# All input projections by seven products, in stages of 1536 and 1024 columns, with one function each for silu and gelu and a planner that alternates late and early passes

## The chip, the cores and the metric

The kernel runs on one core of a Trainium2 chip. Five engines work side by side on that core: PE (TensorE, matrix products into PSUM), VectorE (DVE in the profile), ScalarE (ACT), GpSimd (POOL) and SyncE (SP), which here issues nearly all transfers between DRAM and SBUF. Each engine takes its own instructions in order and waits on semaphores for the others. The metric is the device time of one execution in microseconds; lower is better.

## The reference

One layer of a decoder: 1024 tokens, model width 2048, all in float32. In short:

```python
h = rmsnorm(x, ln_g)
P = h @ w_in                       # 2048 x 6672
g_u, g_v, g_z, d_q, d_k, d_v, d_z, d_a, d_b, c_q, c_z = split(P)
A = gelu(g_u) * (tril(W_s) @ layernorm(gelu(g_v)) + b) * silu(g_z)       # 4 groups x 128
q, k, v = silu(causal_conv(d_q, d_k, d_v))                               # 8 heads x 128 each
B = rmsnorm(gated_delta_rule(l2norm(q), l2norm(k), v, decay(d_a), sigmoid(d_b))) * silu(d_z)
C = softmax(c_q @ mk.T) @ mv * silu(c_z)      # 4 heads, 256 memory tokens, mk, mv = rmsnorm(mem) @ w_mem_kv
y = rmsnorm(x + concat(A, B, C) @ w_out, final_g)
```

The delta rule is a scan over the tokens in chunks, with a triangular inverse for each chunk and a 128x128 state for each head.

## The kernel before

**Products.** A float32 operand is split by `split_to` (line 457) into a rounded part `hi` (ScalarE) and the rest `lo` (VectorE), and a product is three fast products, hi·hi, hi·lo and lo·hi (`triple`, line 480). Tokens are handled as two halves of 512 (`hf`), so a product has 128 columns of weights (or tokens) as its stationary operand and 512 columns moving.

**Stages, in program order.**
1. The memory projection: `w_mem_kv` in 16 steps of k, with the norm of memory and, in between, the norm of x's first half (`prep`, line 572): square sums on ScalarE, a VectorE multiply by row factor and gain, transposes on PE, then split into `ahi`/`alo` (four quarters each, resident) and stored as `h0_d`. The gain was copied to all partitions by `spread_gain` (line 567): four products of a row of ones.
2. Plain products for q, k and v of heads 0 to 3 (`project`, `project_first`, lines 891 and 906): for each head and each token half 16 steps of k with 3 products, the result going straight into the convolution. Weights come in pieces of 128x512; their `lo` is kept in DRAM for the second half (`low_d`). `project_first` does its 48 products as two token halves of 256 columns each, so that it can start before all tokens are normed. Norm and transposes of x's second half (`prep1`, `keep_rows`) and the sums of the two halves (`left_sums`) are jobs on the list `todo`, started one by one behind later products.
3. Five pairs of 512-column blocks (`pairs`: q/k of heads 4 to 7; z of the delta heads; v of heads 4 to 7 with the gating's v; the gating's u and z; attention's z and q) by `seven` (line 1341): Strassen's scheme in Winograd's form. Inputs are the two token halves and the two halves of the model width on one side, the two halves of the width and the two column blocks on the other. Seven products, in the order 2, 1, 6, 5, 3, 7, 4 (the "keys"), each over 8 steps of k and 4 column tiles, replace eight. Keys 2 and 1 take the first token half as it is; 5, 6, 7 and 3 take sums of token halves, kept in DRAM; 4 takes the second half. The weight differences are made on the fly by VectorE (`rights_made`, `minus`). Four PSUM banks hold one product; after a key they are copied or added out (`takes`) while the next key begins.
4. The output projection: two more such pairs, interleaved.

**Side work.** For each pair of heads and token half: `front` (convolution, silu, norms, the chunk's two 128x128 tables), `inverse` (62 small VectorE operations for up to four fronts at once), `levels` (block inverse on PE), `values`, `scan_step` and `heads_out` (together `back`). Heads 0 to 3 did this in one go during stage 2; for heads 4 to 7 `front` stored its tiles in DRAM (`late_d`) and `front_late` read them back some stages later. It uses the PSUM banks `dn0` to `dn3`.

**Functions.** `tanh_gate` and `gelu2` (lines 785 and 792) made silu and gelu from tanh with extra VectorE steps; exp and tanh are the only other looked-up functions.

**Order.** Every call is recorded by `Plan` (line 62) as an operation with an engine, a price and its dependences. `lay` simulates the engines and picks, on each, the ready operation with the lowest key; `latest` sets due times backwards from the order found; three rounds are made and the order with the earliest simulated end is written out. All instructions therefore carry line 312 in the profile, and one goes by tile names.

Of the kernel before, what the change touches and what calls it, by code (L numbers as in the profile page):

```python
# [9 lines left out]
F32 = mybir.dt.float32  # L10
# [28 lines left out]
GELU_C = math.sqrt(2.0 / math.pi)  # L39
GELU_A = 0.044715  # L40
# [8 lines left out]
class Op:  # L49
    __slots__ = ("eng", "fn", "args", "kw", "cls", "idx", "cost", "lat", "nbytes", "lock", "n", "succ", "ready", "at",  # L50
                 "lead", "tail", "wait")
# [11 lines left out]
class Plan:  # L63
# [3 lines left out]
    DMA_RATE = 300.0  # L67
    DMA_FIXED = 1600.0
    SWITCH = 250.0
    SPREAD, PASSES = 1.5, 2  # L70
# [111 lines left out]
    def price(self, o, name, outs, ins):  # L182
# [6 lines left out]
        o.nbytes = o.lock = 0  # L189
        o.lat = 0.0  # L190
        if name == "dma_start":
            o.cost = {"sp": 490.0, "act": 100.0, "pool": 800.0}[o.eng]
            rows = math.prod(out.shape[:-1])
            o.nbytes = max(4 * math.prod(out.shape), 512 * rows)
            src = ins[0]
# [11 lines left out]
        elif o.eng == "act":  # L207
            o.cost = (165.0 if psum else 200.0) + 0.82 * n + (105.0 if pointer else 0.0)
# [14 lines left out]
    def lay(self, key):  # L223
# [5 lines left out]
        dma = 0.0  # L229
# [5 lines left out]
        while left:  # L235
# [14 lines left out]
            head = self.ops[heapq.heappop(now[e])[1]]  # L250
            for o in (head, *head.tail):
# [6 lines left out]
                if o.lock:  # L258
                    held[e] = end
                free[e] = end - min(self.OVERLAP[e], 0.5 * o.cost)  # L260
# [17 lines left out]
        return max(free.values())  # L278
# [21 lines left out]

    def issue(self):
        key, best = [o.cls for o in self.ops], None
        for _ in range(self.PASSES + 1):
            end = self.lay(key)
            if best is None or end < best[0]:
                best = end, [o.at for o in self.ops]
            key = self.latest()
        for o, o.at in zip(self.ops, best[1]):
            pass
        self.ops.sort(key=lambda o: (o.at, o.idx))  # L310
        for o in self.ops:
            o.fn(*o.args, **o.kw)  # L312
# [3 lines left out]
def kernel(  # L316
# [84 lines left out]
    ahq = [C([P, NT, 4, P], f"ahi{q}", F32R) for q in range(NQ)]  # L401
    alq = [C([P, NT, 4, P], f"alo{q}", F32R) for q in range(NQ)]
    for t in (*ahq, *alq):
        R.users[t.tensor.name] = []
    ahi = [ahq[k // 4][:, :, k % 4] for k in range(KT)]
    alo = [alq[k // 4][:, :, k % 4] for k in range(KT)]
    wraw = Ring("wraw", 2, [P, 2 * HT])
    whi = Ring("whi", 2, [P, 2 * HT], dt=F32R)
    wlo = Ring("wlo", 2, [P, 2 * HT], dt=F32R)
    kvraw = [*wraw.bufs]  # L410
    kvhi, kvlo = [*whi.bufs], [*wlo.bufs]
    for r in (wraw, whi, wlo):
        r.bufs = [b[:, i * HT : (i + 1) * HT] for b in r.bufs for i in range(2)]
    whi.bufs.append(C([P, HT], "whi4", F32R))
    wlo.bufs.append(C([P, HT], "wlo4", F32R))
    ring = {t: Slots(t, 4, [P, HT]) for t in ("kT", "qT", "vs", "kd", "ai")}
    ring |= {t: Slots(t, 2, [P, 2 * HT]) for t in ("inv", "gt")}
    ring["ut"] = Ring("ut", 2, [P, 2 * HT])
    ring["zg"] = Ring("zg", 2, [P, 2 * HT])
    zgb = ring["zg"].bufs  # L420
    ring["zg"].bufs = [b[:, i * HT : (i + 1) * HT] for b in zgb for i in range(2)]
# [19 lines left out]
    hT_d = DT([KT, P, HT], "hTd")  # L441
# [18 lines left out]

    def raw_piece(src, cls=4):
        raw = wraw()
        v = raw if src.ndim == 2 else raw.rearrange("p (k c) -> p k c", k=src.shape[1])
        with rank(cls):
            Q.dma_start(v, src)
        return raw

    def split_piece(raw):
        hi, lo = whi(), wlo()
        with rank(2):  # L470
            split_to(hi, lo, raw, V)
        return hi, lo
# [27 lines left out]
    def row_tiles(tag):  # L500
        if tag in ("inv", "gt", "ut"):
            return [b[:, i * HT : (i + 1) * HT] for b in (ring[tag](), ring[tag]()) for i in range(2)]
        return [ring[tag]() for _ in range(4)]

    gb = [ring["zg"]() for _ in range(4)]
    kvraw += [ring["ut"]() for _ in range(2)]
    mem_rows = [row_tiles("kT"), row_tiles("qT")]
# [14 lines left out]
    def load_x(tt, tag, after=(None,) * 4):  # L522
        x_rows[tt] = row_tiles(tag)
# [6 lines left out]
    mrow = rows[0:16]  # L530
    with rank(2):
        load_mem(0)
        S.dma_start(mrow, mem_norm_g[0].rearrange("(c p) -> c p", p=P))
        for c in range(4):
# [1295 lines left out]
```

## Time and profile before

| | |
|---|---|
| median of 3 runs (lowest, highest) | 1628.9 us (1628.83, 1635.46) |
| profiled execution | 1628.64 us |
| its span, first to last instruction | 1626.9 us |
| PE, VectorE, ScalarE busy | 1610.1, 1321.4, 1020.9 us |
| TensorE clock granted | 0.998 of full speed |
| bytes moved by transfers | 419.44 MB |

How to read it: `PE` are products, `PEld` their weight loads, which overlap. A group row has line, engine, operation, out<-in by tile names (digits left out), shape and count, then busy time in us and the mean duration in ns, then the idle time of the engine ahead of the group and what ended it. Products overlap in the pipeline, so their durations add up to more than the time they take; the distance between two starts is the time that one costs. A window row has, for each engine, busy time and count in that stretch, then the granted clock, the mean busy share of the 16 DMA engines and the rate in GB/s. A wait row has the total in us, how often, and the longest.

### The profile page before, as it was taken

The numbers are of one execution on the slowest core, as the hardware profiler recorded it, in microseconds if no ns is written. First come the engines' busy times: TensorE is split into PE (matmuls) and PEld (weight loads), VectorE is DVE, ScalarE is ACT, GpSimd is POOL, SyncE is SP. The second block draws the span as 40 slices with busy tenths as digits, with TensorE's granted clock in tenths as the row PEclk, the third lists the DMA queues.
The fourth block names the chain that finished last, engine by engine and source line by source line (L and its number), as shares of the span: only waits on it lengthen the run. The fifth ranks groups of instructions, "written<-read, shape, count | busy, mean of one in ns | idle before, by whom it ended". The sixth has DMA issues, their size and how long they took to land.

```text
span 1626.9 us, 25678 instructions
## 1 busy us (share of the span) xinstructions
PE 1610.1 (99%) x8570; PEld 1350.2 (83%) x8570; DVE 1321.4 (81%) x2288; ACT 1020.9 (63%) x2235; POOL 100.2 (6%) x139
## 2 busy tenths in 40 slices
PE   8999999999999999999999999999999999999997
PEld 6988888888888888888888888888888888888886
DVE  5865796948879869899999898878768897778875
ACT  6957674676755356967776545766667774444355
POOL 0001100010110000100100100000000000000001
PEclk9999999999999999999999999999999999999999
DMA  8978996887886857689877986989768889688646
GB/s 275 272 229 246 289 275 197 248 246 251 282 271 222 285 200 239 206 279 349 293 234 232 327 260 191 292 294 312 262 208 267 297 288 329 200 276 293 213 148 233
DMA packets 316847, 419.44 MB, mean 258 GB/s; under 512 B 51822, under 2 KB 140583, under 8 KB 316715
## 3 DMA queue, kind: packets, MB, share of 16 engines
q1 hardware_dynamic: 315010, 414.65, 79.0%
q0 software_dynamic: 1088, 2.10, 0.4%
q8 instruction: 67, 1.10, 0.3%
q10 hardware_dynamic: 616, 1.07, 0.2%
q14 instruction: 66, 0.53, 0.1%
HBM read 334.33 MB, written 82.87 MB: 256 GB/s over the span
## 4 chain that ended last, share of the span: by engine, by line
PE 98%; DMA 1%; ACT 0%; DVE 0%; issue 0%; ACTq 0%; DVEq 0%; SPq 0%
PE acc L312 75%; PE dn L312 23%; DMA kT<-in_w_in_dram 0%; DMA ut<-in_x_dram 0%; DMA hTd<-tn 0%; DMA kT<-in_mem_dram 0%; ACT y L312 0%; DVE ut L312 0%; DVE kT L312 0%; DVE kd L312 0%; DVE inv L312 0%; ACT vs L312 0%; ACT whi L312 0%; ACT gt L312 0%; ACTq L312 0%
## 5 line engine op out<-in xcount | busy, mean ns | idle before, releaser
L312 PE MATMUL acc<-ahi,whi 128*128 128x512 f32 (+1 forms) x1152 | 442.6, 393 | 0.2
L312 PE MATMUL acc<-alo,whi 128*128 128x512 f32 (+1 forms) x1152 | 440.9, 392 | 0.0
L312 PE MATMUL acc<-ahi,wlo 128*128 128x512 f32 (+1 forms) x1152 | 404.8, 393 | 0.0
L312 PEld LDWEIGHTS acc<-ahi,wlo 128*128 128x128 f32 x1152 | 216.3, 188 | 41.8
L312 PEld LDWEIGHTS acc<-alo,whi 128*128 128x128 f32 x1152 | 216.4, 188 | 40.6
L312 PEld LDWEIGHTS acc<-ahi,whi 128*128 128x128 f32 x1152 | 216.4, 188 | 40.5 <-ACT whi L312 0.9
L312 PE MATMUL acc<-ahi,zh 128*128 128x512 f32 x736 | 222.6, 395 | 0.0
L312 ACT CAST whi<-wraw 128x512 fp32r<-128x512 f32 (+1 forms) x170 | 136.9, 807 | 118.3 <-PE acc L312 91.5
L312 DVE TENSOR_TENSOR alo<-raws,ahi 128x1024 fp32r<-128x1024 f32 x131 | 159.7, 1220 | 37.3 <-ACT ahi L312 35.9
L312 ACT CAST ahi<-raws 128x1024 fp32r<-128x1024 f32 x131 | 137.4, 1050 | 65.5 <-PE dn L312 27.8
L312 DVE TENSOR_TENSOR wlo<-wraw,whi 128x1024 fp32r<-128x1024 f32 (+1 forms) x138 | 134.8, 979 | 40.3 <-ACT whi L312 36.1
L312 PEld LDWEIGHTS acc<-ahi,zh 128*128 128x128 f32 x736 | 136.6, 188 | 26.6
L312 PE MATMUL acc<-ahi,zl 128*128 128x512 f32 x368 | 129.2, 394 | 0.0
L312 DVE TENSOR_TENSOR ahi<-y,ahi 128x1024 fp32r<-128x1024 f32 x65 | 79.3, 1219 | 17.6 <-ACT ahi L312 17.6
L312 ACT CAST ahi<-y 128x1024 fp32r<-128x1024 f32 x65 | 68.2, 1050 | 36.7 <-PE acc L312 26.6
L312 PEld LDWEIGHTS acc<-ahi,zl 128*128 128x128 f32 x368 | 69.1, 188 | 13.4
L312 ACT CAST zh<-wraw 128x1024 fp32r<-128x1024 f32 x36 | 37.8, 1051 | 40.8 <-PE acc L312 17.1
L312 PE MATMUL dn<-wlo,ahi 128*128 128x512 f32 x152 | 59.1, 389 | 0.0
L312 PE MATMUL dn<-whi,ahi 128*128 128x512 f32 x152 | 59.0, 389 | 0.0
L312 PE MATMUL acc<-whi,ahi 128*128 128x512 f32 x144 | 56.1, 392 | 0.0
L312 PE MATMUL acc<-wlo,ahi 128*128 128x512 f32 x144 | 55.9, 391 | 0.0
L312 DVE TENSOR_TENSOR wlo<-y,whi 128x1024 fp32r<-128x1024 f32 x34 | 41.4, 1219 | 14.9 <-ACT whi L312 14.8
(408 smaller groups left out, 3152.7 us busy)
## 6 DMA issues: line engine op xcount, KB each, us to landing
wraw<-in_w_in_dram SPq DMA_DIRECT2D x86, 512.0 KB
raws<-sd SPq DMA_DIRECT2D x74, 512.0 KB
wraw<-in_w_in_dram SPq DMA_DIRECT2D x96, 256.0 KB
y<-in_w_in_dram SPq DMA_DIRECT2D x42, 512.0 KB
y<-sd SPq DMA_DIRECT2D x38, 512.0 KB
wraw<-in_w_out_dram SPq DMA_DIRECT2D x32, 512.0 KB
raws<-h0d SPq DMA_DIRECT2D x27, 512.0 KB
low<-wlo SPq DMA_DIRECT2D x32, 256.0 KB
```

The costliest lines, as they stand in the source:

```text
L312: o.fn(*o.args, **o.kw)
```

## The change

- **Products.** The plain products are gone. q, k and v of heads 0 to 3, then of heads 4 to 7, then z of the delta heads with the gating's v are three stages of 1536 columns by `seven`: two blocks of 512 and two of 256 side by side, six column tiles and six PSUM banks, weight pieces of 128x1536. The last two pairs and the output projection keep 1024 columns.
- **Start.** The first stage takes `ahi`/`alo` as resident operands for keys 2 and 1; its first two steps of key 2 go as two token halves (`first=2`). Key 2 of the second stage is computed right behind (`ahead`) and kept in DRAM. Norm, transposes and sums of x's second half are now one piece of work, `prep1`, ranked as background; it reads the first half back from `h0_d` in short rows and stores the sums so too.
- **Norm.** The gain is a column (`lcol`) and VectorE applies it behind the transpose; `spread_gain` is gone.
- **Side work.** All eight heads store their front tiles and read them back (`late_d`, `gt_d` for all). The decay tables' exponentials move out of the fronts into `decays` and go through DRAM (`e_d`, `ecs`). Fronts and scan share two PSUM banks, later one each, where they had up to four. Transposes of q and k, and of two heads' outputs, go out singly instead of together.
- **Functions.** silu is `AF.Silu`, gelu `AF.Gelu_apprx_tanh`, with no factors to undo.
- **Order.** The planner knows function tables (a price for a change), short-row transfers and a lead limit on SP, and makes eleven rounds: five early passes, and six with keys from `late`, which lays the work out backwards.

The core of the diff:

```diff
-    DMA_RATE = 300.0
+    DMA_RATE = 340.0
-    SPREAD, PASSES = 1.5, 2
+    FIRST, SPREAD, PASSES, STRETCH, AHEAD = 4, 1.75, 6, 1.25, 2000.0
+    TABLE, HOLD = 1300.0, 6000.0
...
-        for _ in range(self.PASSES + 1):
-            end = self.lay(key)
+        for n in range(self.FIRST + self.PASSES + 1):
+            end = self.lay(key, hold)
...
-            key = self.latest()
+            key, hold = self.latest() if n < self.FIRST else self.late(preds), self.HOLD
...
-            V.scalar_tensor_tensor(xq[q], xq[q], r, gb[q], op0=ALU.mult, op1=ALU.mult)
+            V.tensor_scalar(xq[q], xq[q], r, None, op0=ALU.mult)
...
+        with rank(min(R.cls, 1.5)):
+            V.tensor_tensor(out=tok(o), in0=tok(tp), in1=bc(lcol[q], P), op=ALU.mult)
...
     def prep1(i):
-        load_x(NT + i, "ut")
-        prep(NT + i, lambda q, tp: keep_rows(hT_d, q, i, tp), over(scan_banks))
+        for q in range(2):
+            a, b, c, d, e = (pieces() for _ in range(5))
+            for t, k in ((c, q), (d, q + 2)):
+                Q.dma_start(tok(t), quads(h0_d, k, i))
...
+            V.tensor_tensor(out=e, in0=a, in1=b, op=ALU.add)
+            V.tensor_tensor(out=a, in0=c, in1=a, op=ALU.subtract)
+            V.tensor_tensor(out=c, in0=e, in1=c, op=ALU.subtract)
+            V.tensor_tensor(out=d, in0=d, in1=c, op=ALU.subtract)
+            with rank(4.5):
+                for n, t in ((1, c), (0, e), (3, d), (2, a)):
+                    Q.dma_start(quads(hs_d[n], q, i), tok(t))
+                Q.dma_start(quads(hT_d, q, i), tok(b))
...
-        t = ring["tn"]()
-        S.activation(t, o, AF.Tanh)
-        V.scalar_tensor_tensor(o, t, 1.0, o, op0=ALU.add, op1=ALU.mult)
+        S.activation(o, o, AF.Silu)
...
+    zv = ((HT, (C_DZ + HT, C_DZ)), (HT // 2, (C_V, C_V + HT // 2)))
+    NA = 1
+    def others():
+        for cs, d in zip((heads_of(NJ), zv)[:NA], yu_d):
+            ahead(cs, d)
+    project_stage(heads_of(0), to_heads(0), left=held_left, first_yu=early, first=2, beside=beside, then=others)
+    decays(1, ab1)
...
     with rank(2.6):
-        gdrs = [front(p, hf) for hf in range(2) for p in range(NJ // 2, NJ)]
+        gdrs = [front(p, hf, scan_banks) for hf in range(2) for p in range(2)]
+    project_stage(heads_of(NJ), to_heads(NJ), made=yu_d[0] if NA > 0 else None)
+    inv = inverse(gdrs, "a", 1.9)
+    front_sets = over([own_set])
+    scan_banks, work = [dnr.bufs[0]] * 2, over(dnr.bufs[0:1])
...
+        for hf in range(2):
+            for n in range(2):
+                back_of(n, hf, inv[hf * 2 + n])
+                gdrs.append(front(2 + n, hf, [dnr.bufs[1]] * 2))
...
+    project_stage(zv, gated, made=yu_d[1] if NA > 1 else None)
+    inv = inverse(gdrs, "b", 1.9)
...
+    scan_banks, work = dnr.bufs[0:2], over(dnr.bufs[2:3])
     with rank(2.6):
         for hf in range(2):
-            for p in range(NJ // 2, NJ):
+            for n in range(2):
+                back_of(2 + n, hf, inv[hf * 2 + n])
```

944 lines of the change are left out of this document (487 added, 457 removed).

## The prediction

> **What bounds the kernel now.** I read the page first: span, busy times, the chain that ended last.
>
> ```profile
> span 1626.9 us, 25678 instructions
> PE 1610.1 (99%) x8570; PEld 1350.2 (83%) x8570; DVE 1321.4 (81%) x2288; ACT 1020.9 (63%) x2235; POOL 100.2 (6%) x139
> ...
> DMA packets 316847, 419.44 MB, mean 258 GB/s; under 512 B 51822, under 2 KB 140583, under 8 KB 316715
> ...
> PE 98%; DMA 1%; ACT 0%; DVE 0%; issue 0%; ACTq 0%; DVEq 0%; SPq 0%
> ```
>
> PE is busy for all but 16.8 of 1626.9 us and 98% of the chain is PE. VectorE stands at 81%, ScalarE at 63%, so the first question about any edit is what it does to PE. A busy PE is not proof of a full one, so I asked next for PE's waits and for a stretch of the last projection, where nothing but 512-column products run.
>
> ```profile
> PE dn L312 <- DMA kT<-in_mem_dram: 4.3, 1, 4.3
> PE dn L312 <- DVE ut L312: 1.3, 1, 1.3
> PE dn L312 <- DVE inv L312: 1.2, 1, 1.2
> ```
>
> ```profile
> 1380.00:1580.00 200.00, 200.00 (x884) 165.64 (x884) 158.41 (x217) 89.40 (x127) 0.00 (x0) 1.00 0.69 228
> ```
>
> PE waits 6.8 us in three places, all before 160 us; the rest of its idle time is the start and the end. In the second fence (stretch; then busy time and count of PE, weight loads, VectorE, ScalarE, GpSimd; clock; DMA share; GB/s) 884 products take 200.00 us: one per 0.2262 us, at clock 1.00. That, not the 0.39 us of the duration column, is the price of a product, since durations overlap. Products are the bound: what takes one away takes 0.2262 us off the end as long as its operands come in time.
>
> **The change, part by part.**
>
> *Products.* Heads 0 to 3 of q, k and v are twelve blocks of 128 columns. Before, each takes 16 steps x 3 products for each of two token halves: 12 x 96 = 1152. The five pairs take 7 x 8 x 3 x 4 = 672 each, the output projection twice that. After, three stages of 1536 columns take 7 x 8 x 3 x 6 = 1008 each and two of 1024 take 672: 4368 against 1152 + 3360 = 4512. The output projection is untouched. 144 products fewer are 144 x 0.2262 = **-32.6 us**. Splitting the opening products in two token halves is there before (48 products) and after (72): 24 more pairs of halves, about 0.2 us.
>
> *Small PE work.* The gain row of the norm was spread over the partitions by four products of one row; now it is a column that VectorE multiplies in.
>
> ```profile
> L312 PE MATMUL acc<-ahi,whi 128*128 128x512 f32 x1120 | 433.8, 396 | 0.2
> ...
> L312 PE MATMUL acc<-ahi,abw 128*128 128x512 f32 x32 | 12.9, 404 | 0.0
> ...
> L312 PE MATMUL dn<-ident,ut 128*128 128x128 f32 x64 | 12.5, 272 | 1.3 <-DVE ut L312 1.3
> ...
> L312 PE MATMUL dn<-zg,ones 1*128 1x512 f32 x8 | 4.5, 640 | 0.0
> ```
>
> The eight records of `zg,ones` are 4.5 us busy in a stretch where PE is full: **-4.2 us** with the overlap off. The transposes of x's second half (`ident,ut`, 12.5 us busy) and the decay products (64 records of which 32 are shown) remain. Two transposes for the exponentials of the decays are new. Transposes of q and k, and of two heads' outputs, which went out as one group, go out singly: 24 more changes between full-precision and fast products. What a change costs is in the order of time:
>
> ```profile
> 61.45 0.28 PE L312 MATMUL acc<-gt,whi 128*128 128x256 f32 x1
> 61.57 0.60 PE L312 MATMUL dn<-ident,kT 128*128 128x128 f32 x4
> 61.92 0.37 PE L312 MATMUL acc<-gt,whi 128*128 128x256 f32 x1
> 62.13 0.40 PE L312 MATMUL acc<-inv,whi 128*128 128x256 f32 x2
> ```
>
> The usual distance after a 256-column product is 0.12 us (61.45 to 61.57). Four transposes take 0.35, and the product behind them is 0.21 from its successor: 0.09 more. 24 x 0.09 = **+2.2 us**, and 0.4 for the new transposes. The new order of the planner also regroups everything else. No row shows how; some 110 such groups either way are 10 us, which I keep as a bound on both sides and take at 0.
>
> So the PE floor is 1626.9 - 32.6 - 4.2 + 0.2 + 2.2 + 0.4 = **1592.9 us** of span.
>
> *The start: where transfers are tight.* Before, the plain products of head 0 ran while x's second half was normed in the background, job by job. After, the first stage needs the sums of both halves from its third product (key 6) on. Ahead of that stand three products that need only the first half: keys 2 and 1, and key 2 of the next stage, taken early. When the first of today's products starts (durations, then first and last start):
>
> ```profile
> L312 PE MATMUL acc<-ahi,whi x1152: 274/389/502, 66.8 to 1298.8; 128*128 128x512 f32 x186, 128*128 128x256 f32 x6
> ```
>
> Cover on PE: the memory projection up to 62.6 us (66.8 less 4.2), 3 x 144 x 0.2262 = 97.7, the first half's decays 32 x 0.2262 = 7.2, the second half's transposes 12.5, small work 2: **182 us** to the start of key 6.
>
> What must have moved by then, in tiles of 128x512 (0.262 MB): memory and its weights 40, x 32, first half stored and read back 32, keys and values 8, weights of the three products 12 + 24 + 12, the early result 6, sums 30 (six of eight groups of five, since ten buffers turn round), operands for the first two steps of key 6 10: 206 tiles, **54.0 MB**. The rates of today's early stretches:
>
> ```profile
> GB/s 275 272 229 246 289 275 197 248 246 251 282 271 222 285 200 239 206 279 349 293 234 232 327 260 191 292 294 312 262 208 267 297 288 329 200 276 293 213 148 233
> ```
>
> ```profile
> 0.00:50.00 50.00, 44.49 (x259) 36.77 (x260) 26.47 (x40) 34.88 (x65) 3.56 (x13) 1.00 0.84 277
> 50.00:100.00 50.00, 50.00 (x328) 44.50 (x326) 41.22 (x86) 37.03 (x86) 2.85 (x6) 1.00 0.88 259
> 100.00:150.00 50.00, 50.00 (x255) 41.50 (x254) 33.72 (x72) 37.45 (x104) 5.23 (x6) 1.00 0.78 230
> 150.00:200.00 50.00, 48.67 (x239) 40.25 (x238) 34.26 (x67) 32.54 (x94) 8.12 (x10) 1.00 0.91 280
> 200.00:250.00 50.00, 50.00 (x230) 41.50 (x229) 46.79 (x105) 35.42 (x99) 1.16 (x1) 1.00 0.89 257
> ...
> 1310.00:1617.00 307.00, 307.00 (x1375) 253.98 (x1373) 241.19 (x344) 148.59 (x232) 4.05 (x7) 1.00 0.73 246
> ```
>
> In 50 us stretches the early rates are 230 to 280 GB/s at shares of 0.78 to 0.91; the last fence line (output projection) has 246 at 0.73. At 280, the best of them, 54.0 MB take 193 us, 10.5 more than the cover. Bounds: at 280 / 0.91 = 308 GB/s they take 175 us and no wait arises; at the lowest slice of the page, 229 GB/s, they take 236 us, a wait of 53 us. I take 280: demand here will be steady, as it was there, so **+10.5 us**. Queued behind the wait are all later products, since PE takes its queue in order.
>
> *VectorE and ScalarE.* A 1536-wide split is new; between 512 and 1024 columns the rows rise by 0.535 (VectorE) so one is 1.22 + 0.535 = 1.76 us.
>
> ```profile
> L312 DVE TENSOR_TENSOR alo<-raws,ahi 128x1024 fp32r<-128x1024 f32 x131 | 159.7, 1220 | 37.3 <-ACT ahi L312 35.9 <-DMA y<-in_x_dram 0.3 <-DMA sd<-vs 0.3
> ...
> L312 DVE TENSOR_TENSOR inv<-inv,y 32x31 f32<-32x31 f32 (+25 forms) x155 | 51.4, 331 | 1.7
> ...
> L312 DVE TENSOR_TENSOR y<-acc,y 128x512 f32<-128x512 f32 x64 | 43.5, 685 | 4.0 <-PE acc L312 3.6
> ...
> L312 DVE SCALAR_TENSOR_TENSOR kT<-xr,cw,kT 128x512 f32<-128x512 f32 x48 | 36.1, 752 | 0.8 <-ACT kT L312 0.6
> ...
> L312 DVE SCALAR_TENSOR_TENSOR y<-et,y 128x512 f32<-128x512 f32 x40 | 27.0, 684 | 1.9 <-ACT et L312 1.9
> ...
> L312 DVE TENSOR_TENSOR wraw<-wraw,kd 128x512 f32<-128x512 f32 x24 | 15.9, 683 | 1.9 <-DMA wraw<-in_w_out_dram 1.7 <-DMA wraw<-in_w_in_dram 0.2
> ```
>
> A 1536 stage costs VectorE 28 x (1.22 + 1.76) + 20 x 1.76 + 18 x 0.685 = 131 us against 228 us of PE; a 1024 stage today 28 x 2.44 + 40 x 0.683 + 12 x 0.685 = 104 against 152. Silu and gelu as one function drop the 27.0 us of `y<-et,y`, about 16 of gelu's first steps and 48 x 0.7 = 34 of the convolutions; norming by columns adds 32 x 0.69 = 22. VectorE ends within 3% of 1321 us. No time on the path.
>
> *Side work* (convolutions, inverses, the scan). All eight heads now go through memory between the front part and the scan, and the scan has one or two PSUM banks where it had four.
>
> ```profile
> 500.00:1000.00 500.00, 500.00 (x2425) 417.09 (x2425) 452.94 (x738) 317.28 (x615) 31.42 (x42) 1.00 0.78 255
> 1000.00:1310.00 310.00, 310.00 (x1947) 263.43 (x1946) 252.15 (x405) 213.19 (x497) 14.76 (x21) 1.00 0.84 272
> ```
>
> ```profile
> 1000.00:1250.00 250.00, 28.90 (x176) 25.96 (x176) 8.66 (x28) 7.79 (x32) 1.00 0.84 271
> ```
>
> The last fence is the scan's small tiles alone: four backs run inside 1000 to 1250 us while PE stays full (310.00 of 310.00). After, four backs and four fronts fall into the 1536 stage of gates and values, PE time 228 + some 75 of their own (28.9 for the scan's small tiles, the rest estimated for block inverses, chunk tables and transposes) = 303; VectorE there 131 for the stage, 80 for eight heads' fronts, 48 for four backs (each head's operations counted, at 0.34 to 0.75), 11 for gates and 20 for an inverse (62 steps of 0.33): 290. That is 96%, and from 500 to 1000 it is 453 of 500 today with PE full. What does not fit moves into the two 1024 stages, where VectorE has 58 of 310 us free. Cost 0; without that cover, some 10 to 15 us.
>
> *Queues.* SP issues some 70 transfers more (the four tiles of four heads, the decay tiles; fewer weight pieces), spread over the span; GpSimd's 16 selections move to the decays, where it is 6% busy. Cost 0, but SP is in order: a store that waits for VectorE holds the weight loads behind it, which is inside the 10.5 us.
>
> *Function tables.* Tanh and exp were served by one load; silu, gelu and exp must change tables.
>
> ```profile
> L312 ACT CAST ahi<-raws 128x1024 fp32r<-128x1024 f32 x131 | 137.4, 1050 | 65.5 <-PE dn L312 27.8 <-PE acc L312 22.5 <-issue 14.8
> ...
> L312 ACT COPY y<-acc 128x512 f32<-128x512 f32 x72 | 41.9, 585 | 13.5 <-PE acc L312 13.0
> ...
> L312 ACT ACT_TABLE_LOAD x1 | 1.3, 1283 | 4.0 <-DMA y<-in_mem_norm_g_dram 4.0
> ```
>
> A load is 1.283 us. Between the last product of a bank and the first that reuses it stand 3 x 6 x 0.2262 = 4.07 us with four banks, 6.8 with six. One load, one split and one copy are 1.283 + 1.05 + 0.585 = 2.92: hidden. Up to 68 changes (16 gelu and 16 attention pieces and two decay groups, each alone among silus) are 87 us of ScalarE's 606 idle. Cost 0.
> The Trainium skill, "ScalarE: Activation LUTs", section "What ACT_TABLE_LOAD costs", speaks against the change: every switch costs about 2.66 us with the drain, not the load alone. By that the three would be 4.30 us, 0.23 over the four banks' cover, at most 68 x 0.23 = 16 us more by estimate. The trace of before has one load and no drain beside it, so it cannot decide.
>
> **Sum.** 1592.9 + 10.5 = 1603.4 us of span. The profiled execution took 1628.64, 1.7 more than its span, and the median of the runs is 1628.9, 0.3 above it: 1603.4 + 1.7 = **1605 us**.
>
> **Rivals.** 0.5% (8 us) is about what a measurement here can tell from no change.
>
> *The start starves (slower).* Place: key 6 of the first stage. With early rates of 229 GB/s the wait is 53 us: 1592.9 + 53.4 + 1.7 = 1648. It turns slower than before once the wait passes 34 us, 54.0 MB in 216 us, so below 250 GB/s; one of today's five early stretches lies there and two within 10 of it. Against it: they were not starved for demand, PE was full in them.
>
> *The start costs most of the gain.* At 250 to 263 GB/s, 23 to 34 us of wait: 1618 to 1629.
>
> *No wait at the start.* At 308 GB/s: 1594.6, and down to 1585 with the regrouping bound. For it: the output projection's 246 at 0.73 is 337 at full share. Against: 259 at 0.88 in the stretch where x's first half is stored in short rows is 294.
> The Trainium skill, "DMA: Bandwidth & Descriptors", section "Specifications", has transfers at full rate from 512 B on, which would make this rival the likeliest; the early rows at 294 do not agree.
>
> *Tables on the path.* If each of 68 loads showed whole, 87 us: 1692. Against: it needs every one to meet a bank handover.
>
> *The saving isn't made.* If the wide stages issued as many products as now, the time would be 1605 + 32.6 = 1638; the counts above leave no room, and the trace will show the number.
>
> **How the numbers follow.** Forecast (wait 0 to 23 us) 0.57; no wait or better 0.14; most of the gain lost 0.12; start starves 0.13; tables or no saving 0.04. The range leaves out the best 0.06 and the worst 0.10: 1586 to 1640; the forecast's own is 1592 to 1618. Faster by over 0.5% means below 1620.8: 0.57 + 0.14 + 0.03 = 0.74; within 0.5% (to 1637) 0.11; slower 0.15.
>
> **What would show it.** 144 fewer 512-column records and 0.2262 us still between them; PE waits, if any, at 160 to 220 us, ended by a transfer of sums or weights, DMA share there above 0.9; no `zg,ones`; VectorE within 3% of 1321 us; table loads in the tens, ScalarE waits ended by PE as today. Wrong would make it: PE waits after 250 us, above all in the scan with fewer banks, or distances between products above 0.2262.

## The result and the profile after

The changed kernel takes 1620.26 us (median of 6 runs, 1616.38 to 1621.55), the kernel before 1630.41 beside it: ratio 0.993, 95% interval 0.9912 to 0.9948. That is 10 us gained where 24 were forecast. The profiled execution took 1620.26 us, its span is 1618.5, so it lies 25.6 us over the sum's 1592.9 without the start wait. The page of the changed kernel, the lines that answer to those of before:

```profile
span 1618.5 us, 24604 instructions
PE 1585.5 (98%) x8444; PEld 1327.3 (82%) x8444; DVE 1224.7 (76%) x1794; ACT 953.0 (59%) x1984; POOL 101.6 (6%) x143
...
DMA packets 313759, 429.92 MB, mean 266 GB/s; under 512 B 52249, under 2 KB 138018, under 8 KB 313634
...
PE 77%; DMA 7%; DVE 5%; ACT 3%; issue 2%; SPq 1%; ACTq 0%; DVEq 0%
```

The chain was 98% TensorE and is 77%: transfers, VectorE, ScalarE and SP's queue now hold 16% of it. The work that was to go is gone: 512-column records fall from 6016 to 5848, which is the 144 products and 24 more that are issued as 48 halves, and the `zg,ones` records no longer occur. Nor has a product become dearer where TensorE is full. In such a stretch of the output projection (stretch; busy time and count of TensorE, weight loads, VectorE, ScalarE, GpSimd; clock; DMA share; GB/s) 222 take 50.00 us, 0.225 each:

```profile
1400.00:1450.00 50.00, 50.00 (x222) 41.44 (x221) 36.79 (x38) 19.67 (x25) 0.00 (x0) 1.00 0.73 239
```

So the 25.6 us should for the most part be time in which TensorE stands or runs slowly. The same view by stage, first of the kernel before, then of the changed one:

```profile
0.00:100.00 100.00, 94.49 (x584) 81.27 (x584) 67.69 (x125) 71.91 (x149) 6.41 (x19) 1.00 0.86 268
100.00:400.00 300.00, 298.67 (x1658) 250.30 (x1657) 220.90 (x518) 196.89 (x567) 30.69 (x36) 1.00 0.82 246
400.00:600.00 200.00, 199.82 (x1135) 167.59 (x1134) 164.89 (x289) 114.10 (x238) 12.73 (x16) 1.00 0.80 263
```

```profile
0.00:100.00 100.00, 89.55 (x588) 81.95 (x589) 76.38 (x134) 64.58 (x131) 8.57 (x20) 0.97 0.95 308
100.00:400.00 300.00, 299.52 (x1345) 245.57 (x1345) 198.96 (x237) 132.00 (x197) 14.44 (x25) 1.00 0.84 261
400.00:600.00 200.00, 195.69 (x923) 162.90 (x922) 163.78 (x259) 125.59 (x298) 21.94 (x20) 0.99 0.82 266
600.00:900.00 300.00, 297.14 (x1884) 251.29 (x1883) 231.75 (x379) 220.88 (x595) 28.66 (x40) 1.00 0.83 265
900.00:1300.00 400.00, 399.10 (x2351) 336.33 (x2350) 311.47 (x478) 255.56 (x528) 22.43 (x30) 1.00 0.84 274
1300.00:1600.00 300.00, 296.37 (x1325) 242.84 (x1324) 234.64 (x295) 146.24 (x221) 2.86 (x4) 1.00 0.73 242
```

Length less busy time is TensorE's idle time. Before, it is 5.5 us in the first 100, 1.3 to 400, 0.2 to 600 and nothing from there to 1600: 7.0 us. After, it is 10.5, 0.5, 4.3, 2.9, 0.9 and 3.6: 22.6. To that comes lost clock: one minus the granted clock times busy time, added up over stretches of 10 us, is 0 before and 4.6 us after (3.0 in the first 100, 1.6 between 400 and 600). Idle time and clock explain 15.6 + 4.6 = 20.2 of the 25.6 us. The other 5.4 stay unassigned: 0.6 of them are idle time after 1600 us (10.4 us against 9.8 before), the rest lies in TensorE's busy time. There a product's record lasts 0.40 us and the next one starts after 0.225, so a short wait doesn't show as idle time, and no view here tells it from a dearer small tile.

There is no single wait behind this. TensorE's six longest in the changed kernel (what waited, what ended it, us in total, times, longest):

```profile
PE dn L400 <- DMA kept<-in_mem_dram: 5.7, 2, 4.4
PE dn L400 <- ACT kd L400: 3.3, 1, 3.3
PE dn L400 <- DVE yu L400: 1.6, 1, 1.6
PE dn L400 <- DVE tn L400: 1.5, 1, 1.5
PE dn L400 <- DVE gcol L400: 1.3, 1, 1.3
PE dn L400 <- DVE states L400: 1.3, 1, 1.3
```

Two places of the changed kernel show how waits come about. The first is at 60 to 80 us, in stretches of 1 us:

```profile
65.00:66.00 1.00, 0.40 (x4) 0.20 (x2) 1.00 (x3) 0.87 (x1) 0.00 (x0) 1.00 0.98 293
66.00:67.00 1.00, 0.57 (x5) 0.57 (x6) 1.00 (x3) 1.00 (x3) 0.00 (x0) 1.00 0.97 282
67.00:68.00 1.00, 0.52 (x5) 0.28 (x3) 1.00 (x3) 0.97 (x4) 0.00 (x0) 1.00 1.03 295
68.00:69.00 1.00, 0.00 (x0) 0.00 (x0) 1.00 (x3) 1.00 (x3) 0.00 (x0) 1.00 0.79 141
69.00:70.00 1.00, 0.98 (x5) 0.84 (x5) 1.00 (x1) 0.62 (x2) 0.00 (x0) 0.58 0.72 131
70.00:71.00 1.00, 0.22 (x2) 0.00 (x0) 1.00 (x4) 0.31 (x2) 0.00 (x0) 0.50 0.83 240
...
75.00:76.00 1.00, 1.00 (x6) 1.00 (x6) 1.00 (x3) 0.97 (x3) 0.00 (x0) 0.51 1.09 354
```

VectorE is full (1.00 in each row) while TensorE stands: besides its splits it scales x's rows and multiplies the transposes by the gain, and the last rows' transposes wait for it (three waits, 3.5 us). Then the clock falls to 0.50 and stays there to 76 us. The wait is paid twice, once as idle time and once as products at half speed.

The second is the output projection, where the kernel before had no wait at all. The waits of SP's queue there (1320 to 1480 us), before and after, and a piece of the chain after (start, us, what; `...` stands for steps of 0.02 us):

```profile
SPq L312 <- DVE alo L312: 46.5, 18, 4.9
```

```profile
SPq L400 <- PE acc L400: 28.4, 12, 4.9
SPq L400 <- DVE rlo L400: 27.7, 13, 5.1
```

```profile
1341.40 9.35 DMA ll<-mixd
...
1350.77 1.06 ACT lh L400
...
1351.85 0.27 DVE ll L400
```

Before, a left operand was loaded into a tile of its own, and the next load could be issued as soon as VectorE had split it (`alo`). After, it is loaded into the buffer of its low part (`ll`), and the next load has to wait until TensorE has used that part (`PE acc`). What stands behind in the queue waits as well. From 100 to 1320 us SP's queue waits 221.3 us for TensorE (134.2 on `dn`, 87.1 on `acc`), against 75.8 before. How much of this reaches TensorE is another matter: of its 3.5 us of waits after 1320 us, 1.6 are ended by the split of a left operand.

### The profile page after: what moved, and what is told of

Same layout as the page of the kernel before. It is cut to its first block, busy times and chain, and to the rows that moved or that the text cites. A ratio compares the mean times of both kernels' runs of the same rounds, so it can differ in the third digit from the quotient of the medians.

```text
span 1618.5 us, 24604 instructions
## 1 busy us (share of the span) xinstructions
PE 1585.5 (98%) x8444; PEld 1327.3 (82%) x8444; DVE 1224.7 (76%) x1794; ACT 953.0 (59%) x1984; POOL 101.6 (6%) x143
## 4 chain that ended last, share of the span: by engine, by line
PE 77%; DMA 7%; DVE 5%; ACT 3%; issue 2%; SPq 1%; ACTq 0%; DVEq 0%
PE acc L400 48%; PE dn L400 29%; DMA raw<-in_w_in_dram 2%; DMA ll<-mixd 1%; DMA ll<-sd 1%; DVE rlo L400 1%; ACT lh L400 1%; DVE ll L400 1%; SPq L400 1%; ACT rhi L400 0%; DMA xr<-pd 0%; ACT jk L400 0%; DVE kept L400 0%; DVE raw L400 0%; DMA sm<-mixd 0%
## 5 line engine op out<-in xcount | busy, mean ns | idle before, releaser
L400 PE MATMUL acc<-lh,rhi 128*128 128x512 f32 x1024 | 354.2, 397 | 0.5 <-ACT rhi L400 0.5
L400 PE MATMUL acc<-lh,rlo 128*128 128x512 f32 x1024 | 345.7, 395 | 0.0
L400 ACT CAST rhi<-raw 128x1024 fp32r<-128x1024 f32 (+1 forms) x148 | 186.6, 1261 | 231.0 <-PE dn L400 105.6
L400 DVE TENSOR_TENSOR rlo<-raw,rhi 128x1024 fp32r<-128x1024 f32 (+1 forms) x148 | 220.4, 1489 | 61.9 <-ACT rhi L400 46.6
L400 PE MATMUL acc<-ll,rhi 128*128 128x512 f32 x688 | 238.9, 396 | 0.0
L400 PEld LDWEIGHTS acc<-lh,rlo 128*128 128x128 f32 x1024 | 191.3, 188 | 37.7
L400 PEld LDWEIGHTS acc<-lh,rhi 128*128 128x128 f32 x1024 | 191.1, 188 | 37.7 <-ACT rhi L400 0.7
L400 DVE TENSOR_TENSOR ll<-ll,lh 128x1024 fp32r<-128x1024 f32 x123 | 151.5, 1231 | 51.3 <-ACT lh L400 51.0
L400 ACT CAST lh<-ll 128x1024 fp32r<-128x1024 f32 x123 | 129.2, 1051 | 92.7 <-DMA ll<-mixd 38.4
L400 PEld LDWEIGHTS acc<-ll,rhi 128*128 128x128 f32 x688 | 128.4, 188 | 24.6 <-DVE ll L400 0.4
L400 PEld LDWEIGHTS dn<-lh,rhi 128*128 128x128 f32 x288 | 54.1, 188 | 10.4
```

## Experiments

Where a sentence gives idle time and clock, they are read as above, from the kernel's profiled run, up to 1600 us unless it says otherwise.

### Is it the body or the scheduler?

Four candidates stood at this point: the new order of instructions, the shallower operand buffers, VectorE's share of the start, and the function tables. The first two runs cross body and scheduler.

```
-class Plan: (early passes)          # e1: body of before,
+class Plan: (early and late passes) #     scheduler of after
```

> The kernel before, with nothing changed but the scheduler: the alternate late and early passes and their constants. Three theories for the 25.6 us that the changed kernel lies over the floor of 1592.9 us. Order: the new scheduler places the side work worse; then this kernel is slower than the kernel before (1630.4) by 10 to 25 us, 1640 to 1655. Body: the loss belongs to the new stages and buffers, and the scheduler is neutral; then 1627 to 1634. Order helps: the new scheduler by itself hides part of the 16.8 us of TensorE idle time of before; then 1615 to 1625.

1637.31 us (ratio 1.0038, 1.0021 to 1.0054): slower than before by 6 us, less than the order theory asked for and more than the body theory.

```
-class Plan: (early and late passes) # e2: body of after,
+class Plan: (early passes)          #     scheduler of before
```

> The changed kernel, with the scheduler of before put back (three early passes, no account of function tables, transfers planned at 300 instead of 340 GB/s). Order: if the new scheduler is what loses the time, this one is faster than the changed kernel (1620.3), 1598 to 1612. Body: if the new stages lose it whatever the order, it stays within 5 us, 1615 to 1625. Order helps: if the new order only mends part of what the stages lose, it is slower than the changed kernel, 1630 to 1660, and the count of function table loads is above 21.

1707.28 us (1.0458, 1.043 to 1.0486). Without its own scheduler the new body is 87 us slower. 19 table loads occur, so these are not the matter. TensorE's idle time is 76.1 us and lost clock 27.0. 41 us of the idle time lie in three stretches, where TensorE waits for tiles of the scan and of the gates (9.4 us for `sq` from memory, 9.0 for ScalarE's `os`, 6.4 for its `vs`), at a clock of 0.63 to 0.79:

```profile
840.00:880.00 40.00, 27.66 (x220) 23.19 (x219) 25.92 (x58) 29.66 (x104) 3.84 (x6) 0.79 0.75 249
920.00:950.00 30.00, 14.88 (x63) 11.30 (x63) 17.54 (x39) 22.05 (x73) 2.81 (x4) 0.69 0.77 261
1060.00:1090.00 30.00, 16.16 (x134) 13.83 (x132) 13.24 (x20) 8.80 (x17) 3.01 (x4) 0.63 0.77 209
```

Which part of the scheduler does it:

```
-    FIRST, SPREAD, PASSES, ... = 4, 1.75, 6, ...
+    FIRST, SPREAD, PASSES, ... = 10, 1.75, 0, ...   # e10
```

> The changed kernel with all eleven passes of its scheduler early ones, no late pass, everything else of it (function tables counted, transfers at 340 GB/s) kept. With the old scheduler whole, the changed kernel took 1707 us. If it is the late passes that spread the side work of the scan over the products, this one lies near that, 1680 to 1710, with TensorE waiting for ScalarE and VectorE at the ends of the stages. If it is the model of transfers, 1620 to 1640.

1630.45 us (1.0004, 0.9992 to 1.0015). The late passes are worth 10 us, not the 60 or more of the first theory. The bound on the loading queue:

```
-    ... STRETCH, AHEAD = ..., 1.25, 2000.0
+    ... STRETCH, AHEAD = ..., 1.25, 1.0e9            # e15
```

> The changed kernel, without the one line of its scheduler that holds the loading queue back when it is over 2 us ahead of the transfers. With the old scheduler whole, the changed kernel took 1707 us, with early passes alone and the rest new 1630. If this line is what makes the rest of the difference, this one lies between 1650 and 1700; if it is elsewhere (the assumed rates, the late passes), within 1612 to 1630.

1635.16 us (1.0032, 1.0016 to 1.0047), 15 us; between the two theories. One wait of 11.0 us in the first stage, for the decays' VectorE work, is most of it:

```profile
PE dn L400 <- DVE sc L400: 11.7, 2, 11.0
```

10 and 15 do not make 87, and the 10 are hardly more than what the order moves by chance (next). The rest (the price of short rows, the bookkeeping of the loading queue) was not taken apart and stays open.

How much is the order's chance? One constant, the assumed transfer rate, deals the order out anew:

```
-    DMA_RATE = 340.0
+    DMA_RATE = 330.0     # e7;  320.0 in e11
```

> A control: the changed kernel with the scheduler's assumed transfer rate at 330 instead of 340 GB/s, which alone deals the whole order out anew. It shows how far the time moves by the order's chance. If under 3 us (1617 to 1624), differences of other kernels by more than that come from their edits; if 5 us or more, single edits inside the changed kernel say little below that.

> A second control: the changed kernel with the scheduler's assumed transfer rate at 320 GB/s. At 330 it took 1611.9 us, 8.4 us less than at 340. If these differences are chance of the order, this one lies anywhere from 1608 to 1625; if a slower assumed rate is a truer one (loads are ordered earlier), it lies at 1612 or below.

330 gives 1611.87 us (0.9879, 0.9861 to 0.9897) and 320 gives 1616.97 (0.9917, 0.9903 to 0.9932). Neither is truer than the other: 340, 330 and 320 give 1620, 1612 and 1617. A single edit that moves the time by less than some 8 us can't be told from this by the time alone, so the following runs are read by their stages first. At 330 the waits after 1320 us are 0.8 us where the changed kernel has 3.5, with the same buffers, and SP's queue waits longer for TensorE than at 340, 252.8 us against 221.3, from 100 to 1320:

```profile
SPq L400 <- PE dn L400: 159.3, 91, 6.7
SPq L400 <- DVE rlo L400: 113.4, 68, 4.5
SPq L400 <- PE acc L400: 93.5, 50, 4.9
```

So a long wait in the queue is no price by itself. It is one when the load behind it comes too late for its product.

### Function tables

```
+            if o.tab > 1:                            # e4
+                o.args = (*o.args[:2], AF.Tanh, *o.args[3:])
```

> The changed kernel in the same order of instructions, with silu and gelu computed as a plain tanh, which leaves these two functions out of the result (the gates' values are then other ones), so that no other table is needed than that of exp. Table theory: the 21 loads of function tables, 26.9 us of ScalarE, stand in the way of evictions and splits; without them the time falls by 5 to 15 us, to 1605 to 1615. Rival (the prediction's cost of nothing): they lie in ScalarE's 665 us of free time, one or two loads remain, and the time stays within 2 us of 1620.3.

```
-FITS = {AF.Exp: 1, AF.Silu: 2, AF.Gelu_apprx_tanh: 3}
+FITS = {}                                            # e16
```

> The changed kernel, with its scheduler blind for function tables (none has a price, none is held back). The prediction's rival of 1692 us had up to 68 loads at 1.283 us on ScalarE, on TensorE's path. If grouping by the scheduler is what keeps them few, the count rises from 21 to 40 to 68 and the time by 5 us or more, 1625 or above; if the functions come in groups anyway, 19 to 30 loads and 1612 to 1625.

The loads of the changed kernel and of the first of these two:

```profile
L400 ACT ACT_TABLE_LOAD x21 | 26.9, 1283 | 2.6 <-PEq L1871 1.7 <-DVE small L400 0.6
...
L402 ACT ACT_TABLE_LOAD x1 | 1.3, 1283 | 1.7 <-PEq L1873 1.7
```

With one load instead of 21, in the same order, the time is 1620.71 us (0.9931, 0.9912 to 0.995), the same. With a scheduler that is blind for tables there are 21 loads all the same, and 1616.98 us, inside the order's chance. A price of the tables on TensorE's path doesn't show, within the interval of some 3 us either way, and the functions come in groups by themselves.

### The start

```
-        if q in (0, 1, 2, 3):          # on VectorE
+        if q in ():                    # e3: all on ScalarE
```

> The changed kernel, with the multiplication of x's rows by their reciprocal norm on ScalarE instead of VectorE (32 instructions of 128x512). Start theory: the first product starts at about 71 us instead of 62.6 because VectorE, busy 91 to 95% from 50 to 80 us, holds the transposes of the normed rows; then TensorE's idle time from 60 to 80 us falls from 3.5 us to under 1 us, and the time by 2 to 6 us, to 1614 to 1618. Rival: ScalarE (83 to 98% busy there) is as short, the wait moves from one engine to the other, and the time stays within 2 us of 1620.3 or grows.

```
-            V.tensor_scalar(xq[q], xq[q], r, None, op0=ALU.mult)
+            pass                       # e14
```

> The changed kernel without the multiplication of x's rows by their reciprocal norm, which leaves the norm out of the result. 32 instructions of 128x512 on VectorE go, 16 of them ahead of the first product, some 6 to 10 us of its time there. Start theory: TensorE waits from 60 to 80 us because VectorE and ScalarE, both over 90% busy, are short; then TensorE's idle time and lost clock from 0 to 100 us (10.5 and 3.0 us in the changed kernel, 5.5 and 0 in the kernel before) fall to about 7 and 0, and the time to 1610 to 1616. Rival: the wait there comes from the load of x's last rows or of the memory's rows; then both numbers stay, and the time stays within the order's chance, 1612 to 1625, with no fall in the first 100 us.

The first 100 us of the kernel with ScalarE, and of the one without the multiplication:

```profile
0.00:100.00 100.00, 91.29 (x611) 82.84 (x612) 70.45 (x115) 81.48 (x159) 8.36 (x21) 1.00 0.99 321
```

```profile
0.00:100.00 100.00, 92.35 (x618) 83.72 (x619) 70.83 (x112) 63.35 (x122) 7.67 (x19) 1.00 0.95 310
...
400.00:600.00 200.00, 192.40 (x908) 160.57 (x908) 161.54 (x263) 126.11 (x298) 17.25 (x20) 0.98 0.80 257
```

Idle time and lost clock there fall from 13.5 us to 8.7 and to 7.6. The second is the start theory's value; in the first, TensorE's idle time from 60 to 80 us falls from 3.5 to 1.9 us, where that theory asked for less than 1. VectorE's work on x's rows is what TensorE stood for. Yet the times are 1619.6 (1613.59 to 1621.23) and 1620.86, above what the theory forecast in both. The profiled execution of the first kernel is its fastest, 1613.59 us, so its stages don't show what its other executions lost. In the second one sees where it went: the new order loses 9.4 us between 400 and 600 where the changed kernel lost 5.9, and 3.5 between 900 and 1300 instead of 0.9.

Whether the wait for transfers that the prediction put at key 6 is there underneath:

```
-    NA = 1
+    NA = 0                             # e13
```

> The changed kernel without the early product of the second stage: its 12 row pairs of m = 2 stand at that stage's own place, and the first stage keeps 96 fewer products ahead of its key 6. The prediction's step: transfers of 54 MB have to land before key 6, at 280 GB/s, and the cover of products decides whether TensorE waits there. By that step the cover is shorter by 96 times three products of 0.2262 us or less, and a wait of tens of us appears between 120 and 200 us, ended by a transfer: 1635 or more. Rival: transfers run at over 300 GB/s and what key 6 needs comes first in the queue, there is no wait to uncover, and the time stays between 1612 and 1625, the chance of the order.

1621.38 us (0.994, 0.9923 to 0.9958). The early product is 144 products, 32.6 us of cover (the expectation misstates their number). Without it key 6 starts at 161.9 us instead of 187.7, and TensorE is still full where the wait should be, here from 100 to 200 us:

```profile
100.00:200.00 100.00, 100.00 (x467) 82.59 (x467) 72.68 (x98) 34.63 (x50) 3.06 (x5) 1.00 0.92 276
```

It loses 18.8 us in the first 100 instead of 13.5, and less further on.

### Operand buffers

```
-        raw = load2(araw(), src)                        # e5, in before
-        return split2(raw, ah4(), al4())
+        load2([lo.bitcast(F32)], src)
+        return split2([lo.bitcast(F32)], ah4(), lo)
-    whi3 = over([*kvhi, heir(zgb[0], ...)])             # lo, raw alike
+    whi3 = over([*kvhi])
```

> The kernel before with the changed kernel's buffering of the projections and nothing else of it: left operands loaded straight into the buffer of their low part (three of these, two of the high part, no separate raw tiles), right operands with two raw, two high and two low buffers instead of three each. Supply theory: the changed kernel loses its time because a load now waits until TensorE has finished with the buffer (SP's queue waits 221 us for TensorE from 100 to 1320 us, where the kernel before waits 76 us) and what stands behind that load in the queue comes late; then this kernel is slower than the kernel before (1630.4) by 8 to 25 us, 1638 to 1655. Rival: two deep is enough, since a pair of rows is used for 6 us by 24 products and a load takes 5 to 7 us; then 1628 to 1634.

1669.21 us (1.0225, 1.0205 to 1.0245): 38 us slower, beyond the supply theory's 25. In the output projection this is shallower than the changed kernel, which adds a third buffer there for the left and right high parts and the right low parts (`oh`, `rs`), so the 38 us are more than a price of the changed kernel's buffers. (Its last product of the output projection holds three row pairs back with two buffers, so some operands of that product are overwritten; the work is the same. In e8 below this holds for the low parts.) SP's queue now waits for TensorE 304.6 us from 100 to 1320 us, most of them on `acc`:

```profile
SPq L312 <- PE acc L312: 261.2, 140, 9.6
```

Does the new order make it bearable?

```
+class Plan: (early and late passes) # e9: e5 with the scheduler of after
```

> The kernel before with the shallow buffering of e5_before_two_deep and, besides, the changed kernel's scheduler. As in that kernel, the last product of the output projection holds three row pairs back while two buffers of the high part exist, so part of its operands are overwritten and that product is wrong; the work is the same. By itself the scheduler cost the kernel before 5.8 us, the shallow buffering 38 us. Supply theory (the new order is what makes shallow buffers bearable): the sum of the two does not hold, the time is 1635 to 1650. Rival: the scheduler has nothing to do with the buffers, the two prices add up, 1670 to 1680.

1671.06 us (1.0251, 1.0226 to 1.0275). No: the rival held, the price stays.

```
-    lefts_lo = over([*halves(own(alq[2], ...)), own(ah3[0], "lm", ...)])
+    lefts_lo = over([*halves(own(alq[2], ...))])         # e8
```

> The changed kernel with one buffer fewer for left operands: two of the low part instead of three. Supply theory: the depth of these buffers is what TensorE waits on; then a third less costs about as much again as has been lost, 15 to 40 us, 1635 to 1660, with SP's queue waiting longer for TensorE than 221 us from 100 to 1320 us. Rival, side work: TensorE waits for transposes and scan steps between the products, the operands come in time anyway; then under 5 us, 1620 to 1625.

1670.92 us (1.0239, 1.0221 to 1.0256). One left buffer fewer costs 51 us, more than the supply theory said. Up to and after 900 us:

```profile
100.00:900.00 800.00, 790.29 (x4119) 652.64 (x4118) 582.71 (x851) 479.13 (x1077) 60.71 (x82) 1.00 0.80 258
900.00:1669.40 769.40, 726.46 (x3757) 593.77 (x3755) 567.44 (x808) 416.22 (x780) 35.52 (x40) 0.99 0.76 250
```

The changed kernel after 900 us, and the longest waits of TensorE in the kernel with one buffer fewer that splits of operands end:

```profile
900.00:1618.50 718.50, 703.60 (x3709) 585.56 (x3707) 553.86 (x788) 409.96 (x764) 27.96 (x38) 1.00 0.80 262
```

```profile
PE dn L400 <- DVE ll L400: 8.7, 3, 8.0
PE acc L400 <- ACT lh L400: 8.2, 11, 2.1
PE dn L400 <- ACT oh L400: 7.2, 4, 3.4
```

TensorE's idle time is 9.7 us up to 900 us and 42.9 after, here to the end of the span; the changed kernel's is 7.7 (from its stages above) and 14.9. Splits of left operands (`ll`, `lh`) end 21.9 us of its waits and splits into `oh`, which serves both sides, another 11.6; in the changed kernel splits of left operands end 2.1 and none into `oh`. In all the idle time grows by 31.9 of the 51 us; most of the rest lies in TensorE's busy time, 1604.5 us against 1585.5. The buffer is missed in the stages of 1024 columns, where a pair of rows is used by 24 products or 5.4 us, far more than in those of 1536, where it is used by 36 or 8.1. That the width is what makes shallow buffers bearable fits these rows, but no run changed the width alone.

```
-        return loaded(two(mix2_d[...]))                   # e6
+        return apart(two(mix2_d[...]))   # raw tiles: kept[i][:, 1024:1536]
```

> The changed kernel, with left operands loaded into separate tiles in the output projection alone (two pairs of 512 columns, in the unused last third of the four kept buffers) and split from there, as the kernel before did. Supply theory: the waits of TensorE from 1350 to 1460 us (3.5 us, behind loads of left operands that take 6.4 to 9.4 us and were issued late) go, and TensorE's excess over even spacing there, 6 us, with them: 1613 to 1617, waits after 1320 us under 1 us in all. Rival, transfers: the loads are slow because many run at once (DMA share 0.9 there), not because they are issued late; then the waits stay, and the time stays within 2 us of 1620.3.

1612.34 us (0.9886, 0.9866 to 0.9906). The time is a little under what the supply theory asked for, but waits of 3.1 us after 1320 remain, and the order of 330, which has the changed kernel's buffers, has 0.8 there. None of the 3.1 is ended by the split of a left operand any more; the longest is another:

```profile
PE acc L400 <- DVE gt L400: 2.0, 1, 2.0
```

This gain can't be told from the order's chance. Depth costs dearly when it goes, and in this projection more of it brought nothing that another order doesn't.

### A version that beats both?

```
-    DMA_RATE = 340.0
+    DMA_RATE = 330.0                   # e12, e17 and e18
-        if q in (0, 1, 2, 3):
+        if q in (0, 2):                # e12 (with e6's edit), e17
+        if q in ():                    # e18
-            S.activation(xq[q], xq[q], AF.Copy, scale=r)
+            G.tensor_scalar(xq[q], xq[q], r, None, op0=ALU.mult)   # e17
```

> The changed kernel with three edits: rate at 330 GB/s, left operands of the output projection loaded apart, and the multiplication of x's rows shared between VectorE and ScalarE (quarters 0 and 2 on VectorE). If waits of the output projection and of the start are separate from the order's chance, it gains on 1611.9 by 3 to 6 us, 1605 to 1609. If the order of 330 already hides what the two other edits mend, 1610 to 1615.

> The changed kernel at 330 GB/s (1611.9 us), with two of four quarters of x's rows multiplied by the norm on GpSimd instead of VectorE. Start theory, as the kernel without the multiplication showed it: with half of it off VectorE, TensorE's idle time and lost clock from 0 to 100 us (10.0 and 3.1 us at 330) fall by 2 to 5 us, and, if the order loses nothing elsewhere, the time is 1607 to 1610. Rival: what is saved at the start is lost by the new order further on, as in that kernel, and the time is 1610 to 1618; or GpSimd, slower, delays the rows and the first 100 us lose more.

> The changed kernel at 330 GB/s with the whole multiplication on ScalarE. At 340 this edit took the loss of the first 100 us from 13.5 to 8.7 us in the profiled run and left the median where it was. Start theory: the first 100 us lose 8 to 9 us again and the time is 1606 to 1610. Rival, chance of the order: 1610 to 1618, with the start mended and other waits in the stages after.

1611.44 us, 1611.33 and 1610.84, against 1611.87 for 330 alone; each lies about 1.2% below the kernel before (e18: ratio 0.9887, 0.9862 to 0.9912) and half a per cent below the changed one, and among themselves they can't be told apart. On ScalarE the first 100 us again lose less, 9.4 us instead of 13.1, but the total doesn't follow. With GpSimd they lose 14.3: slower, as its rival said.

## Why the prediction was wrong

The saved products came. Two kinds of step failed: the start wait, whose transfer rate was taken too low, so that no wait came where it was put, and terms that were put at nothing or left out, above all VectorE's work at the start, side work, the order and the clock.

*Products and small work* held: the records, the distance of a product (0.225 us) and the missing `zg,ones` are as said. The terms of 2.2 and 0.4 us can't be seen by themselves.

*The start wait (+10.5)* failed as a mechanism, and its size was right only by accident. No transfer holds TensorE at key 6, which starts at 187.7 us; from 100 to 400 us it idles 0.5 us. The mis-sized figure is the rate. The sum took 280 GB/s; up to key 6 it was 294, and at 294 the 54.0 MB take 183.7 us, about the cover of 182:

```profile
0.00:187.70 187.70, 177.25 (x991) 153.75 (x992) 133.59 (x210) 90.60 (x167) 11.53 (x26) 0.98 0.95 294
```

Even with the early product gone no wait appeared, at 302 GB/s up to its key 6. (The sum's own terms, 192.9 less 182.0, give 10.9 and not 10.5, and its 229 GB/s is the lowest of the page's first slices, not of the page, which goes down to 148.) The Trainium skill, "DMA: Bandwidth & Descriptors", section "Specifications", which has full rate from 512 B on, spoke for that rival; the first 100 us, 308 GB/s at a share of 0.95 or 324 at full share, agree with it better than the 280 I took. What is lost at the start, 8.0 us more than before, is lost 100 us earlier, most of it to VectorE (5.9 us come back without the multiplication). The step "VectorE and ScalarE" looked at VectorE's total, which fell to 1224.7 us (7%, not within 3%; the terms that the step lists, 77 us off and 22 on, are already 4%); it should have looked at the stretch in which it has no slack.

*Side work at no cost* failed: 400 to 900 us has 7.2 us of idle time and 1.6 of lost clock, where before had 0.2; the longest waits there are for tiles of the side work (`kd` 3.3, `states` 1.3, `os` 1.2). The sentence that priced it without cover at 10 to 15 us was near. That the few PSUM banks are the reason was not shown by any run.

*The output projection is untouched* failed: its products are, its left buffers aren't. In-place loading stands in the diff, not in the description of the change, and was given no price. TensorE idles 3.6 us there, but these are not shown to come from it: with separate tiles waits of 3.1 us remained, and at 330, with the same buffers, 0.8. What is shown is that the kernel stands near an edge, since less depth cost 38 to 51 us.

*Regrouping, taken at 0* failed as a single value. Its bound of 10 us either way was about right: three constants spread over 8.4 us, and the drawn order was the worst of the three. The prediction treated the scheduler as neutral; the new body takes 87 us more without it.

*Clock* was missing from the sum: 4.6 us. The gap of the spans closes so: 1618.5 - 1603.4 = 15.1, made of 15.6 of idle time in place of 10.5, 4.6 of clock and 5.4 unassigned. That removing these losses one by one would bring the forecast was not shown: what the start gained, later stages lost again, and the lowest median of any run is 1610.84 us.

*Function tables and queues at no cost* held for the tables, by two runs, as far as 3 us can be told. For SP's queue it holds only with the order at hand.

## What to carry to other kernels

When a change takes work off an engine that is 99% busy, price every buffer that it makes shallower or shares: ask who must finish before the next load may be issued, the splitter or the engine that bounds. Look for a helper engine's slack in the shortest stretch with a deadline, not in its total. Where a scheduler deals the order out, run it at two or three constants before a difference under 1% is given a cause.

## What the runs showed of the hardware

The granted clock in 1 us rows is 1.00 or 0.50, with mixtures where a row spans a change. It halved after 65 to 69 us, although no wait there is longer than 1.5 us: four rows with 0.40, 0.57, 0.52 and 0.00 us busy were enough, and it stayed at half for 6.8 us. The Trainium skill, "TensorE: Matmul & The Clock Gate", section "What's actually happening", has half speed after an idle window of about 3.4 us and full speed again after one busy one. The two values agree. The stretch shows that the window need not be wholly idle; full speed came back at 76 us, some 5 us after TensorE's last gap.

A change of function tables costs ScalarE 1.30 us. In the changed kernel (start, us, engine, operation):

```profile
996.15 1.05 ACT L400 CAST lh<-ll 128x1024 fp32r<-128x1024 f32 x1
997.22 1.28 ACT L400 ACT_TABLE_LOAD   x1
998.51 0.63 ACT L400 ACTIVATE tn<-tn 128x512 f32<-128x512 f32 x1
999.16 1.28 ACT L400 ACT_TABLE_LOAD   x1
```

The load starts 0.02 us after the instruction before it has ended, and the next one starts 0.01 us after the load. The Trainium skill's 2.66 us a switch, which the prediction weighed ("ScalarE: Activation LUTs", "What ACT_TABLE_LOAD costs"), includes a drain that doesn't show here. The 16 us that followed from it were for 68 changes; the 21 loads, at the same 0.23 us each, would be 5, and the run with one load shows none of them.
